# B11+B12 of the fast weight products made by an accumulating DMA in six duos, made first everywhere else, and the last two units of a product swapped

## The chip, the cores and the metric

The kernel runs on one core of one Trainium2 chip. The metric is the device time of one execution in microseconds. Engines are named as the profile names them: PE (TensorE matmul), PEld (its weight load), DVE (VectorE), ACT (ScalarE), POOL (GpSimd), SP (SyncE, which issues nearly all DMAs).

## The reference

A decoder trunk of two layers on 256 tokens, width 2048, in float32. Layer 0 mixes with gated linear attention, layer 1 with differential attention over one shared K/V; each is followed by a SwiGLU feed-forward network (FFN) of width 5632.

```python
def swiglu(h, w_gate_up, w_down):
    gate, up = jnp.split(h @ w_gate_up, 2, axis=-1)
    return (jax.nn.silu(gate) * up) @ w_down
...
        x = x + rmsnorm(mix, post_mix_g[i])
        f = swiglu(rmsnorm(x, pre_ffn_g[i]), ffn_w_gate_up[i], ffn_w_down[i])
        x = x + rmsnorm(f, post_ffn_g[i])
```

## The kernel before, in words

All weights are streamed once from HBM, in pieces of 128 x 1024 floats (512 KB, tile `raw`, line 258). One list, `weight_stream`, gives the order of the whole program. A piece goes through three stations. SP loads it into one of `NRAW` = 5 buffers. ACT rounds it to `hi` (line 294), and DVE subtracts to get `lo` (line 296); both halves go into one of `NRING` = 9 places. PE then makes three products of each pair: a_hi w_hi, a_hi w_lo, a_lo w_hi (lines 370 to 372 and 442 to 444), so that the result has about float32's precision. `pump` converts up to nine pieces ahead of PE and loads up to five pieces ahead of the conversion. The 256 tokens are two blocks of 128.

**Duos.** Where two column chunks c1 and c2 of a weight are computed together (in the FFN: gate chunk c and up chunk 11 + c), some of the eight row pairs s of the chunk are "fast". There the 2 x 2 block product (two token blocks, two column chunks, two row blocks k1, k2) is made in seven block products instead of eight, Strassen-Winograd's way. The fast rows are `FAST_FFN` = 0, 2, 3, 4, 6 (for chunk 1 four of them), and other lists in the mixers. With B11, B21 the halves of the first piece r1 (k1 and k2 of c1) and B12, B22 those of the second piece r2, a fast row gives four units:

- "a": r1 as loaded, two products (banks 0 and 1)
- "b": r2 after the sums, two products (banks 6 and 2)
- "c": r1 after the sums, two products (banks 4 and 3)
- "d": the narrow sum of 128 x 512, one product (bank 5)

The four additions of 128 x 512 run on DVE in `sums` (line 317): B11+B12 over the first half of r1, B12+B22 over the first half of r2, then B11+B12+B22 into the narrow tile `sum`, then that plus B21 over the second half of r1. Behind the last fast row `early` combines banks 0, 5, 6 and 4, and `late` the rest.

**The order on an engine.** The program is recorded in the order of the stream and then put in order by a scheduler that simulates the engines and respects buffers and priorities, so rows of an engine can move when something elsewhere changes. Each engine runs its rows in that order and waits at each for what it needs.

**The stages.** In the trace: gated linear attention (0 to 296 us), its output projection (to 384), FFN 0 (to 1085), values, keys and queries (to 1390), the second output projection `diff_w_out` (to 1468) and FFN 1 with `w_gu1` and `w_d1` (to the end). In an FFN the chunks alternate with down projections. Between the projection and the FFN stands a norm: sums of squares on ACT and DVE, the power -1/2 on POOL (line 625), then transposes on PE and the split of the normed input into `h_ffn` (line 647).

Of the kernel before, what the change touches and what calls it, by code (L numbers as in the profile page):

```python
# [11 lines left out]
F32 = mybir.dt.float32  # L12
# [3 lines left out]
ALU = mybir.AluOpType  # L16
AX = mybir.AxisListType

P = 128
# [3 lines left out]
C = 512  # L23
# [22 lines left out]
CHAIN = (3, 4, 5, 6)  # L46
FIRST_X = {1: [(1, 0), (0, 1)], 3: [(1, 1)], 5: [(0, 2)], 7: [(1, 2)], 9: [(0, 3)], 11: [(1, 3)]}
NRAW, NRING = 5, 9
V_BEGIN, V_EVERY, V_Q = 16, 3, 1


# [29 lines left out]
def weight_stream():  # L81
# [40 lines left out]

    middle_duo("gla_w_out", FAST_OUT)
    ffn(0)
    chunk("w_v", 0)
    chunk("w_v", 3)
    duo(("w_v", 1), ("w_v", 2), FAST_V)
    for name in ("w_k", "diff_w_q"):
        for n in range(KT):
            block(name, n)  # L130
    middle_duo("diff_w_out", FAST_OUT)
    ffn(1)
    return out


def load_list(stream):
    out = []
    for name, idx, kind in stream:
        if kind in ("plain", "beside"):
            out.append((name, idx))  # L140
        elif kind == "a":
            out.extend((name, (n, idx[2])) for name, n in idx[:2])
    return out


class Split:


    def __init__(self, tiles):
        self.tiles = tiles  # L150
# [36 lines left out]
class Trunk:  # L187
    def __init__(self, ctx, tc, t):
        self.ctx, self.tc, self.nc, self.t = ctx, tc, tc.nc, t

        def pool(name, **kw):
            return ctx.enter_context(tc.tile_pool(name=name, bufs=1, **kw))

        self.const = pool("const")
        self.big = pool("big")
        self.ring = pool("ring")
        self.hs = pool("hs")
        self.psum = pool("psum", space=bass.MemoryType.PSUM)
        self.dram = pool("dram", space=bass.MemoryType.DRAM)
        self.n = 0  # L200
        self.later = []
        self.stream = weight_stream()
        self.loads = load_list(self.stream)
        self.n_used = self.n_done = 0
        self.subs = {}
        self.raws = {}
        self.n_dma = self.n_conv = self.n_take = self.n_free = 0
        self.pool_lo = set()
        self.n_narrow = 0
        self.cap = 2  # L210
        self.ident = self.const.tile([P, P], F32, tag="ident", name="ident")
# [44 lines left out]
    def load(self):  # L256
        name, idx = self.loads[self.n_dma]
        raw = self.ring.tile([P, 1024], F32, tag="raw", name=self.uid("raw"), bufs=NRAW)
        self.nc.sync.dma_start(raw, self.t[name][idx])
        self.raws[self.n_dma] = raw  # L260
        self.n_dma += 1

    def raw(self):
# [43 lines left out]
        )  # L307
        return hi

    def sums(self):  # L310

        nc = self.nc
        r1, r2 = self.pending
        t2 = self.narrow[0].tile([P, C], F32, tag="sum", name=self.uid("sum"))

        def add(out, in0, in1):
            nc.vector.tensor_tensor(out=out, in0=in0, in1=in1, op=ALU.add)  # L317

        add(r1[:, :C], r1[:, :C], r2[:, :C])
        add(r2[:, :C], r2[:, :C], r2[:, C:])  # L320
        add(t2, r1[:, :C], r2[:, C:])
        add(r1[:, C:], t2, r1[:, C:])
        self.pending = r1, r2, t2

    def convert(self):
        n = self.n_conv
        kind = self.stream[n][2]
        self.n_done += kind in ("plain", "beside", "c", "b")
        if kind == "plain":
            self.subs[n] = self.split(self.raw(), n in self.pool_lo) if n else self.split_halves(self.raw())  # L330
        elif kind == "beside":
            self.subs[n] = self.split_beside(self.raw())
        elif kind == "a":
            self.pending = self.raw(), self.raw()
            self.subs[n] = self.split(self.pending[0])
        else:
            if kind == "b":
                self.sums()
            self.subs[n] = self.split(self.pending["cbd".index(kind)])
        self.n_conv += 1  # L340

    def pump(self):
# [103 lines left out]
    def duo_act(self, aT, forms, fast, c1, c2, early, late):  # L446

        ps = [self.acc() for _ in range(6)] + [self.tp().rearrange("p j t -> p (j t)")]
        for s in range(8):
            k1, k2 = 2 * s, 2 * s + 1  # L450
            if s in fast:
                f = forms.pairs.index(s)
                plan = {
                    "a": ((0, (k1, 0)), (1, (k2, 0))),
                    "b": ((6, (f, 2)), (2, (f, 3))),
                    "c": ((4, (f, 0)), (3, (k2, 1))),
                    "d": ((5, (f, 1)),),
                }
                first, last = s == fast[0], s == fast[-1]
                for kind, prods in plan.items():  # L460
                    wp = self.take("duo", (c1, c2, s), kind)
                    for j, (bank, (i, which)) in enumerate(prods):
                        plain = kind == "a" or bank == 3
                        a = aT.tokens(i, which) if plain else forms.fast(i, which)
                        stop = last and bank in (0, 5, 6)
                        self.triple(ps[bank], a, wp, j, first, stop)
                    self.free()
                    if kind != "d":
                        self.tick()
                if last:  # L470
                    early(ps)
                continue
            for (w, n), pair in ((c1, ((1, 0), (3, 1))), (c2, ((4, 1), (2, 2)))):
                wp = self.take(w, (n, s))
                for bank, which in pair:
                    for j in range(2):
                        a = forms.diff(k1 + j) if which == 2 else aT.tokens(k1 + j, which)
                        self.triple(ps[bank], a, wp, j, False, s == 7 and j == 1)
                    if s == 7:
                        late(bank, ps)  # L480
                    if bank in (2, 3):
                        self.free()
                    self.tick()

    def duo_apart(self, aT, forms, fast, chunks, early, late):

        ps = {}

        def add(bank, a, wp, j, last):
            first = bank not in ps  # L490
            if first:
                ps[bank] = self.acc() if bank < 6 else self.tp().rearrange("p j t -> p (j t)")
            self.triple(ps[bank], a, wp, j, first, last)

        for s in range(8):
            k1, k2 = 2 * s, 2 * s + 1
            if s not in fast:
                for (w, n), banks in zip(chunks, ((1, 3), (2, 7))):
                    wp = self.take(w, (n, s))
                    for b, bank in enumerate(banks):  # L500
                        for j in range(2):
                            add(bank, aT.tokens(k1 + j, b), wp, j, s == 7 and j == 1)
                        if b:
                            self.free()
                        if s == 7:
                            late(bank, ps)
                        self.tick()
                continue
            f, last = forms.pairs.index(s), s == fast[-1]
            plan = {  # L510
                "a": ((0, aT.tokens(k1, 0)), (1, aT.tokens(k2, 0))),
                "b": ((6, forms.fast(f, 2)), (2, forms.fast(f, 3))),
                "c": ((4, forms.fast(f, 0)), (3, aT.tokens(k2, 1))),
                "d": ((5, forms.fast(f, 1)),),
            }
            for kind, prods in plan.items():
                wp = self.take("duo", (*chunks, s), kind)
                for j, (bank, a) in enumerate(prods):
                    add(bank, a, wp, j, last and bank in (0, 4, 5, 6))
                self.free()  # L520
                if kind != "d":
                    self.tick()
            if last:
                early(ps)
# [632 lines left out]
    def ffn(self, fp, hT, rs, gi, wgu, wd, post, after, name, reload, side=None):  # L1157
        nc = self.nc
        self.narrow, self.n_narrow = (fp, 0, 3), 0
        forms = Forms(FAST_FFN, range(8), self.whole(4, [P, 4, 2, 4, P], f"{name}_fast", F32R))  # L1160
        self.rest_of(forms, 2 * gi + 1, f"{name}_rest")
        temp = self.whole(5, [P, 4, C], f"{name}_temp")
# [48 lines left out]
        f = []  # L1211
# [372 lines left out]
```

## Time and profile before

| | |
|---|---|
| two timed runs | 2179.7 and 2179.91 us, median 2179.8 |
| span of the profiled execution, first to last instruction | 2177.2 us |
| what lies around the span (median less span) | 2.6 us |
| PE, DVE, ACT, POOL busy | 99%, 89%, 58%, 2% |
| DMA engines busy with SP's queue | 60.2% |

The profile gives no time of its own for the profiled execution beside its span, so the runs' median stands for it. Busy PE in this profile is modelled (matmuls overlap), so the number of matmuls in a stretch tells more than the share.

### The profile page before, as it was taken

What the parts mean: (1) busy time and instruction counts of PE and PEld (TensorE: products, weight loads), DVE (VectorE), ACT (ScalarE), POOL (GpSimd) and SP (SyncE); (2) the same over time, 40 slices, a digit from 0 to 9 for tenths busy, and PEclk for the clock granted to TensorE, in tenths of its full rate; (3) what the DMA queues carried; (4) which work ended last, traced back from release to release, by engine and by line L of the source; (5) the groups of instructions that cost most, each with busy time, mean ns of one, the idle gap of its engine ahead of it and who ended that gap; (6) DMA issues with size and microseconds to landing.
All of it is one profiled execution on the core that took longest, in us unless ns stands there. A gap on an engine that the chain in (4) does not pass through costs nothing.

```text
span 2177.2 us, 28399 instructions
## 1 busy us (share of the span) xinstructions
PE 2162.6 (99%) x10098; PEld 1798.1 (83%) x10098; DVE 1932.7 (89%) x2646; ACT 1267.2 (58%) x1744; POOL 35.6 (2%) x66
## 2 busy tenths in 40 slices
PE   9999999999999999999999999999999999999998
PEld 8887788888888888888878888888888888888886
DVE  7989988998999999998898567889999999999986
ACT  8656665665655555554676455556566555555553
POOL 1000000000000000000000000000000000000000
PEclk9999999999999999999999999999999999999999
DMA  8545566666655566665757655465656555666664
GB/s 309 169 149 191 177 228 213 213 221 215 228 176 199 194 213 213 194 224 189 243 187 248 186 174 161 151 235 189 231 194 223 182 185 195 209 206 212 212 213 135
DMA packets 123315, 440.09 MB, mean 202 GB/s; under 512 B 13899, under 2 KB 16628, under 8 KB 121380
## 3 DMA queue, kind: packets, MB, share of 16 engines
q1 hardware_dynamic: 121996, 436.44, 60.2%
q10 hardware_dynamic: 1176, 1.84, 0.3%
q8 instruction: 79, 1.29, 0.2%
q14 instruction: 64, 0.52, 0.1%
HBM read 429.82 MB, written 9.97 MB: 202 GB/s over the span
## 4 chain that ended last, share of the span: by engine, by line
PE 96%; DVE 2%; DMA 1%; issue 1%; ACT 1%; POOL 0%; SPq 0%; DVEq 0%; POOLq 0%; ACTq 0%
PE acc L444 13%; PE acc L443 13%; PE acc L442 13%; PE acc L372 10%; PE acc L370 10%; PE acc L371 10%; PE acc L585 8%; PE acc L586 4%; PE tp L443 3%; PE tp L444 3%; PE tp L442 3%; PE tp L606 1%; DVE lo L296 1%; PE acc L1307 0%; PE acc L1346 0%
## 5 line engine op out<-in xcount | busy, mean ns | idle before, releaser
L294 ACT CAST hi<-raw 128x1024 fp32r<-128x1024 f32 x905 | 929.5, 1051 | 656.6 <-DVE raw L317 272.7
L296 DVE TENSOR_TENSOR lo<-raw,hi 128x1024 fp32r<-128x1024 f32 x903 | 1077.6, 1220 | 151.8 <-ACT hi L294 148.9
L370 PE MATMUL acc<-hi,f_ffn_gT 128*128 128x512 f32 x704 | 274.1, 390 | 0.0
L371 PE MATMUL acc<-lo,f_ffn_gT 128*128 128x512 f32 x704 | 274.0, 390 | 0.0
L372 PE MATMUL acc<-hi,f_ffn_gT 128*128 128x512 f32 x704 | 268.9, 389 | 0.0
L444 PE MATMUL acc<-hi,h_ffn 128*128 128x512 f32 x666 | 259.6, 390 | 0.0
L443 PE MATMUL acc<-lo,h_ffn 128*128 128x512 f32 x666 | 259.2, 389 | 0.0
L442 PE MATMUL acc<-hi,h_ffn 128*128 128x512 f32 x666 | 258.4, 390 | 0.0
L372 PEld LDWEIGHTS acc<-hi,f_ffn_gT 128*128 128x128 f32 x704 | 132.2, 188 | 27.3
L370 PEld LDWEIGHTS acc<-hi,f_ffn_gT 128*128 128x128 f32 x704 | 132.2, 188 | 27.2
L371 PEld LDWEIGHTS acc<-lo,f_ffn_gT 128*128 128x128 f32 x704 | 132.2, 188 | 27.0
L444 PEld LDWEIGHTS acc<-hi,h_ffn 128*128 128x128 f32 x666 | 125.0, 188 | 26.5 <-issue 0.6
L443 PEld LDWEIGHTS acc<-lo,h_ffn 128*128 128x128 f32 x666 | 125.1, 188 | 25.9
L442 PEld LDWEIGHTS acc<-hi,h_ffn 128*128 128x128 f32 x666 | 125.0, 188 | 25.9
L585 PE MATMUL acc<-h_q,hi 128*128 128x512 f32 x256 | 92.5, 401 | 0.0
L585 PE MATMUL acc<-h_kv,hi 128*128 128x512 f32 x256 | 90.6, 399 | 0.0
L585 PE MATMUL acc<-h_mix,hi 128*128 128x512 f32 x256 | 90.5, 398 | 0.0
L317 DVE TENSOR_TENSOR raw<-sum,raw 128x512 f32<-128x512 f32 x122 | 84.2, 690 | 3.5
L317 DVE TENSOR_TENSOR raw<-raw 128x512 f32<-128x512 f32 x122 | 84.2, 690 | 3.3
L317 DVE TENSOR_TENSOR raw<-raw,raw 128x512 f32<-128x512 f32 x122 | 83.9, 687 | 2.0
L317 DVE TENSOR_TENSOR sum<-raw,raw 128x512 f32<-128x512 f32 x122 | 83.5, 684 | 0.0
L586 PE MATMUL acc<-h_q,lo 128*128 128x256 f32 x256 | 73.2, 286 | 0.0
(416 smaller groups left out, 3912.4 us busy)
## 6 DMA issues: line engine op xcount, KB each, us to landing
raw<-in_w_gu_dram SPq DMA_DIRECT2D x352, 512.0 KB, 4.4
raw<-in_w_d_dram SPq DMA_DIRECT2D x176, 512.0 KB, 5.2
raw<-in_gla_w_r_dram SPq DMA_DIRECT2D x32, 512.0 KB, 4.4
raw<-in_gla_w_v_dram SPq DMA_DIRECT2D x32, 512.0 KB, 4.0
raw<-in_gla_w_out_dram SPq DMA_DIRECT2D x32, 512.0 KB, 4.5
raw<-in_w_v_dram SPq DMA_DIRECT2D x32, 512.0 KB, 4.7
raw<-in_w_k_dram SPq DMA_DIRECT2D x32, 512.0 KB, 4.0
raw<-in_diff_w_q_dram SPq DMA_DIRECT2D x32, 512.0 KB, 3.5
```

The source lines that it names most:

```text
L294: nc.scalar.copy(hi, src)
L296: eng.tensor_tensor(out=lo, in0=src, in1=hi.bitcast(F32), op=ALU.subtract)
L317: nc.vector.tensor_tensor(out=out, in0=in0, in1=in1, op=ALU.add)
L370: nc.tensor.matmul(ps, ah, rh, start=(kt == 0), stop=False)
L371: nc.tensor.matmul(ps, ah, rl, start=False, stop=False)
L372: nc.tensor.matmul(ps, al, rh, start=False, stop=(kt == 2 * ns - 1))
L442: nc.tensor.matmul(ps, ah, wh, start=first, stop=False)
L443: nc.tensor.matmul(ps, ah, wl, start=False, stop=False)
L444: nc.tensor.matmul(ps, al, wh, start=False, stop=last)
L585: nc.tensor.matmul(ps, lh, aT.both(kt), start=(kt == 0), stop=False)
L586: nc.tensor.matmul(ps[:, SEQ:], ll, aT.hi(kt), start=False, stop=(kt == KT - 1))
L606: nc.tensor.transpose(tp[:, j, :], src[:, j * P : (j + 1) * P], self.ident)
```

## The change

In the duos of FFN 1 with chunks 2 to 7, the sum B11+B12 is not made by DVE any more. Behind the load of r2 the program issues two more DMAs: SP loads B11 into a narrow tile `sumd` (128 x 512, five buffers), and POOL issues an accumulating DMA that adds B12 from HBM into it. That is 30 fast rows (six duos with five each). Everywhere else DVE makes B11+B12 in kind "a", ahead of the split of r1, in a narrow tile of its own (`sum`, now one buffer in the pool of the ring). The other sums stay in place: B12+B22 in r2, then t1 + B22 over the first half of r1, then that plus B21. So unit "c" now holds B11+B12+B22 where it held B11+B12, and the narrow unit "d" holds B11+B12: the banks 4 and 5 of the two units swap. No matmul is added or removed.

```diff
+SUM_BY_DMA, SUM_CHUNKS = ("w_gu1",), (2, 3, 4, 5, 6, 7)
...
+def summed_loads(stream):
+
+    out, n = {}, 0
+    for name, idx, kind in stream:
+        if kind == "a":
+            (w1, c1), (w2, c2), s = idx
+            if w1 in SUM_BY_DMA and c1 in SUM_CHUNKS:
+                out[n + 1] = ((w1, (c1, s)), (w2, (c2, s)))
+            n += 2
+        elif kind in ("plain", "beside"):
+            n += 1
+    return out
...
         self.raws[self.n_dma] = raw
+        if self.n_dma in self.t1_at:
+            (w1, i1), (w2, i2) = self.t1_at[self.n_dma]
+            t1 = self.more.tile([P, C], F32, tag="sumd", name=self.uid("sumd"), bufs=5)
+            self.nc.sync.dma_start(t1, self.t[w1][i1][:, :C])
+            self.nc.gpsimd.dma_start(t1, self.t[w2][i2][:, :C], accum_op=ALU.add)
+            self.t1s[self.n_dma] = t1
         self.n_dma += 1
...
-    def sums(self):
-
-        nc = self.nc
-        r1, r2 = self.pending
-        t2 = self.narrow[0].tile([P, C], F32, tag="sum", name=self.uid("sum"))
-
-        def add(out, in0, in1):
-            nc.vector.tensor_tensor(out=out, in0=in0, in1=in1, op=ALU.add)
-
-        add(r1[:, :C], r1[:, :C], r2[:, :C])
-        add(r2[:, :C], r2[:, :C], r2[:, C:])
-        add(t2, r1[:, :C], r2[:, C:])
-        add(r1[:, C:], t2, r1[:, C:])
-        self.pending = r1, r2, t2
+    def add(self, out, in0, in1):
+        self.nc.vector.tensor_tensor(out=out, in0=in0, in1=in1, op=ALU.add)
+
+    def convert_fast(self, kind):
+
+        if kind == "a":
+            r1, r2 = self.raw(), self.raw()
+            t1 = self.t1s.pop(self.n_used - 1, None)
+            if t1 is None:
+                t1 = self.ring.tile([P, C], F32, tag="sum", name=self.uid("sum"), bufs=1)
+                self.add(t1, r1[:, :C], r2[:, :C])
+            self.pending = r1, r2, t1
+            return self.split(r1)
+        r1, r2, t1 = self.pending
+        if kind == "b":
+            self.add(r2[:, :C], r2[:, :C], r2[:, C:])
+            self.add(r1[:, :C], t1, r2[:, C:])
+            self.add(r1[:, C:], r1[:, :C], r1[:, C:])
+            return self.split(r2)
+        return self.split(r1 if kind == "c" else t1)
...
-        elif kind == "a":
-            self.pending = self.raw(), self.raw()
-            self.subs[n] = self.split(self.pending[0])
         else:
-            if kind == "b":
-                self.sums()
-            self.subs[n] = self.split(self.pending["cbd".index(kind)])
+            self.subs[n] = self.convert_fast(kind)
...
-                    "c": ((4, (f, 0)), (3, (k2, 1))),
-                    "d": ((5, (f, 1)),),
+                    "c": ((5, (f, 1)), (3, (k2, 1))),
+                    "d": ((4, (f, 0)),),
...
-                "c": ((4, forms.fast(f, 0)), (3, aT.tokens(k2, 1))),
-                "d": ((5, forms.fast(f, 1)),),
+                "c": ((5, forms.fast(f, 1)), (3, aT.tokens(k2, 1))),
+                "d": ((4, forms.fast(f, 0)),),
...
+        self.more = fp
```

The line numbers of the changed kernel are larger: line 296 is 318 there, 317 is 333, and line 625 is 648. Three places show how rows move.

**DVE, one fast row in a summed duo of FFN 1** (the last fast row of chunk 3). Before, with r1 = `raw_14740`, r2 = `raw_14788`:

```order
L317 TENSOR_TENSOR raw_14740<-raw_14740,raw_14788 128x512
L317 TENSOR_TENSOR raw_14788<-raw_14788 128x512
L317 TENSOR_TENSOR sum_14847<-raw_14740,raw_14788 128x512
L317 TENSOR_TENSOR raw_14740<-sum_14847,raw_14740 128x512
L296 TENSOR_TENSOR lo_14853<-raw_14788,hi_14852 128x1024
L296 TENSOR_TENSOR f_ffn_rest<-sum_14847,f_ffn_rest 128x512
L296 TENSOR_TENSOR lo_14862<-raw_14740,hi_14861 128x1024
```

Of the change, with r1 = `raw_14751`, r2 = `raw_14797`:

```order
L333 TENSOR_TENSOR raw_14797<-raw_14797 128x512
L318 TENSOR_TENSOR lo_14850<-raw_14751,hi_14849 128x1024
L318 TENSOR_TENSOR f_ffn_rest<-sumd_14799,f_ffn_rest 128x512
L318 TENSOR_TENSOR lo_14863<-raw_14797,hi_14862 128x1024
L333 TENSOR_TENSOR raw_14751<-sumd_14799,raw_14797 128x512
L333 TENSOR_TENSOR raw_14751<-raw_14751 128x512
L318 TENSOR_TENSOR f_ffn_rest<-sumd_14978,f_ffn_rest 128x512
L318 TENSOR_TENSOR lo_14872<-raw_14751,hi_14871 128x1024
```

Three additions stand where four stood, spread among the splits, and the split of the narrow unit (`f_ffn_rest`, which is taken from `sumd`) has moved ahead of the additions; the one of the next duo's first row (`sumd_14978`) is already here.

**SP and POOL at the end of `diff_w_out`.** SP before, the last loads of that weight and the first of FFN 1's:

```order
L259 DMA raw_12851<-in_diff_w_out_dram 128x1024
L259 DMA raw_12863<-in_diff_w_out_dram 128x1024
L259 DMA raw_12875<-in_diff_w_out_dram 128x1024
L259 DMA raw_12887<-in_w_gu_dram 128x1024
L259 DMA raw_12896<-in_w_gu_dram 128x1024
```

SP of the change, the same place:

```order
L275 DMA raw_12851<-in_diff_w_out_dram 128x1024
L280 DMA sumd_13930<-in_w_gu_dram 128x512
L275 DMA raw_12863<-in_diff_w_out_dram 128x1024
L280 DMA sumd_14028<-in_w_gu_dram 128x512
L280 DMA sumd_14097<-in_w_gu_dram 128x512
L280 DMA sumd_14157<-in_w_gu_dram 128x512
L275 DMA raw_12875<-in_diff_w_out_dram 128x1024
L280 DMA sumd_14275<-in_w_gu_dram 128x512
L275 DMA raw_12887<-in_w_gu_dram 128x1024
L275 DMA raw_12896<-in_w_gu_dram 128x1024
```

POOL before had nothing between the last head's norms (`st_12543`, `st_12548`) and the post-norm of `diff_w_out`; of the change:

```order
L648 TENSOR_TENSOR st_12545<-st_12545,mhalf 128x1
L648 TENSOR_TENSOR st_12550<-st_12550,mhalf 128x1
L281 DMA sumd_13930<-in_w_gu_dram 128x512
L281 DMA sumd_14028<-in_w_gu_dram 128x512
L281 DMA sumd_14097<-in_w_gu_dram 128x512
L281 DMA sumd_14157<-in_w_gu_dram 128x512
L281 DMA sumd_14275<-in_w_gu_dram 128x512
L648 TENSOR_TENSOR st_13060<-st_13060,mhalf 128x1
L648 TENSOR_TENSOR st_13212<-st_13212,mhalf 128x1
L648 TENSOR_TENSOR rs_ffn_0_13318<-st_13319,mhalf 128x1
L648 TENSOR_TENSOR rs_ffn_1_13423<-st_13424,mhalf 128x1
L281 DMA sumd_14454<-in_w_gu_dram 128x512
```

The five tiles of the first summed duo are loaded and summed far ahead of their use, as soon as their memory is free; POOL's two powers of the post-norm (`st_13060`, `st_13212`) now stand behind five accumulating DMAs. Each of the other 25 loads stands where a buffer of the duo before comes free.

**DVE at the start of `diff_w_out`'s duo**, beside the softmax of the last head (`s_0`, `s_1`, the tiles that PE transposes next). Before:

```order
L296 TENSOR_TENSOR lo_12484<-raw_12217,hi_12483 128x1024
L1329 SCALAR_TENSOR_TENSOR s_0_12397<-s_0_12397,st_12399 128x128
L1324 RECIPROCAL st_12408<-st_12408 128x2
L296 TENSOR_TENSOR lo_12510<-raw_12268,hi_12509 128x1024
L1325 TENSOR_TENSOR st_12408<-st_12408,lam_st 128x1
L1326 TENSOR_SCALAR s_1_12406<-s_1_12406,st_12408 128x256
L1329 SCALAR_TENSOR_TENSOR s_1_12406<-s_1_12406,st_12408 128x256
L296 TENSOR_TENSOR lo_12539<-raw_12319,hi_12538 128x1024
```

Of the change, from the same row on, with nine rows of the last two heads left out of the middle (first piece, then second):

```order
L318 TENSOR_TENSOR lo_12484<-raw_12217,hi_12483 128x1024
L333 TENSOR_TENSOR sum_12538<-raw_12319,raw_12381 128x512
L333 TENSOR_TENSOR raw_12381<-raw_12381 128x512
L318 TENSOR_TENSOR lo_12510<-raw_12268,hi_12509 128x1024
L1335 TENSOR_TENSOR s_0_12397<-acc_12394,bias_12347 128x256
L1339 TENSOR_REDUCE st_12399<-s_0_12397 128x2
L1335 TENSOR_TENSOR s_1_12406<-acc_12403,bias_12347 128x512
L644 TENSOR_SCALAR st_12431<-st_12385 128x1
L318 TENSOR_TENSOR f_mix_rest<-sum_12538,f_mix_rest 128x512
```

```order
L1349 TENSOR_TENSOR st_12408<-st_12408,lam_st 128x1
L1350 TENSOR_SCALAR s_1_12406<-s_1_12406,st_12408 128x256
L318 TENSOR_TENSOR lo_12541<-raw_12319,hi_12540 128x1024
L1353 SCALAR_TENSOR_TENSOR s_1_12406<-s_1_12406,st_12408 128x256
```

Two additions, the split of the narrow unit and one wide split have moved ahead of the last step of that softmax, because the sum is now made as soon as both pieces are there.

More of the change, by code (lines that the diff above doesn't have):

```diff
@@ L205, in __init__ @@
         self.subs = {}
+        self.t1s, self.t1_at = {}, summed_loads(self.stream)
         self.raws = {}
```

## The prediction

> **What bounds the kernel now.** I read the page first (span, engines, granted clock, the chain that ended last), then the stretch of FFN 1 in which the change acts, then who waits for whom.
>
> ```profile
> span 2177.2 us, 28399 instructions
> PE 2162.6 (99%) x10098; PEld 1798.1 (83%) x10098; DVE 1932.7 (89%) x2646; ACT 1267.2 (58%) x1744; POOL 35.6 (2%) x66
> PEclk9999999999999999999999999999999999999999
> PE 96%; DVE 2%; DMA 1%; issue 1%; ACT 1%; POOL 0%; SPq 0%; DVEq 0%; POOLq 0%; ACTq 0%
> ```
>
> PE is busy 99% and makes 96% of the chain, at the full granted clock. DVE, with 89%, comes second. Busy PE is modelled, so I ask for the stretch from 1490 to 2150 us (all duos and down projections of FFN 1 but the ends) and for PE's waits over the whole run:
>
> ```profile
> core 0: us, PE busy (x) PEld busy (x) DVE busy (x) ACT busy (x) POOL busy (x), PEclk, DMA share, GB/s
> 1490.00:2150.00 660.00, 660.00 (x2960) 547.41 (x2959) 613.69 (x739) 371.80 (x429) 0.00 (x0) 1.00 0.61 203
> ```
>
> ```profile
> PE acc L372 <- DVE h_ffn L647: 1.2, 4, 0.3
> PE acc L693 <- POOL ones L718: 1.1, 1, 1.1
> PE acc L370 <- ACT h_kv L645: 1.0, 1, 1.0
> PE acc L372 <- DVE h_kv L647: 0.9, 3, 0.4
> PE tp L641 <- DMA x_in<-in_x_dram: 0.7, 1, 0.7
> PE acc L370 <- ACT diff_oT L1370: 0.7, 1, 0.7
> PE acc L371 <- DVE lo L287: 0.2, 1, 0.2
> ```
>
> In 660 us PE issues 2960 matmuls, one per 0.223 us, and the list of waits for that stretch is empty. All of PE's waits in the run are 5.8 us, at the start and at the norms between stages; none is for a sum of a duo. DVE is at 613.69 / 660 = 93%, close, but it isn't waited for.
>
> How far are the conversions ahead of PE?
>
> ```profile
> ACT hi L294 <- DVE raw L317: 126.2, 35, 5.5
> ACT hi L294 <- PE acc L444: 24.9, 16, 3.4
> ACT hi L294 <- PE acc L372: 17.9, 18, 1.7
> ```
>
> 34 times in this stretch ACT waited for PE to free a place, which happens when all nine are full. Nine units hold at least 9 x 6 = 54 matmuls, so a full ring is some 54 x 0.223 = 12 us of work for PE (an estimate; narrow units make it less). ACT's largest wait, 126.2 us for the sums, eats of this lead in the fast rows and never to its end.
>
> **The change part by part.** *1. Thirty additions leave DVE.*
>
> ```profile
> L317 DVE TENSOR_TENSOR sum<-raw,raw 128x512 f32<-128x512 f32 x49 | 33.5, 684 | 0.0
> L296 DVE TENSOR_TENSOR lo<-raw,hi 128x1024 fp32r<-128x1024 f32 x304 | 361.7, 1220 | 32.0 <-ACT hi L294 30.8 <-PE acc L372 0.6
> ```
>
> 30 x 0.684 = 20.5 us of DVE time in six duos. PE waits there 0 us, so on the path this is worth 0. It lengthens the lead of the conversions only. What ends each duo late is next the same as now: PE's own 9966 program matmuls, unchanged.
>
> *2. Thirty plain and thirty accumulating loads, 256 KB each.* SP's part first:
>
> ```profile
> L259 SPq DMA_DIRECT2D raw<-in_w_gu_dram x162: 327/328/776, 1491.1 to 2102.3; - x162
> SPq L259 <- DVE lo L296: 525.6, 244, 9.9
> q1 hardware_dynamic: 121996, 436.44, 60.2%
> gain<-in_post_ffn_g_dram SPq DMA_DIRECT2D x2, 256.0 KB, 3.0
> ```
>
> 30 x 0.33 = 10 us of issuing, on a queue that spends 525.6 us waiting for raw buffers: hidden. The 25 later loads wait for the last reader of a `sumd` buffer, the addition into r1; the split of r1 that frees the next raw buffer stands behind it on DVE, so the raw loads queued behind wait no longer than now. 436.44 MB took 60.2% of 2177 us, so 16 engines move 333 GB/s, and 256 KB take 0.8 us. The accumulation is not in the trace: bounds are 0.8 us of all engines (a plain load, the lowest) and 3.0 us (the 256 KB gain's whole time to landing, the nearest row above); I take 1.6, reading HBM and the tile. Then five fast rows bring 5 x (0.8 + 1.6) = 12 us of DMA work, and a summed duo is 5 x 21 + 3 x 24 = 177 matmuls with 96 of down projections beside it, 273 x 0.223 = 61 us of PE, of which 39%, 24 us, are free. Hidden, and each tile is asked for when the duo before has used it, some 50 us ahead.
>
> *3. The first five, at the end of `diff_w_out`.* Here there is no such room:
>
> ```profile
> 1430.00:1440.00 10.00, 10.00 (x46) 8.29 (x45) 8.62 (x10) 6.32 (x6) 0.00 (x0) 1.00 0.97 356
> 1440.00:1450.00 10.00, 10.00 (x46) 8.29 (x45) 10.00 (x14) 7.08 (x11) 0.00 (x0) 1.00 0.91 320
> 1450.00:1460.00 10.00, 10.00 (x46) 8.29 (x45) 3.80 (x9) 1.37 (x5) 0.00 (x0) 1.00 0.46 163
> 1430.51 8.16 SPq L259 DMA_DIRECT2D raw<-in_diff_w_out_dram  x6
> 1440.08 7.26 SPq L259 DMA_DIRECT2D raw<-in_w_gu_dram  x5
> ```
>
> SP issues them between 1435 and 1440 us into engines that are 97% busy, so their 12 us push the last two `diff_w_out` pieces (by the plain ones ahead of them, 0.8 to 3.3 us, and what the first accumulations take) and the first `w_gu1` pieces (by up to 12 us). The lead of a full ring is 12 us, and the next 10 us use 46% only. I cost it at 0, with 12 us as its bound.
>
> POOL's powers of the post-norm stand behind the five accumulations:
>
> ```profile
> 1403.17 2.46 POOL L625 TENSOR_TENSOR st<-st,mhalf 128x1 f32<-128x1 f32 x2 [13.30 <-DVE st L621]
> 1460.56 0.55 POOL L625 TENSOR_TENSOR st<-st,mhalf 128x1 f32<-128x1 f32 x1 [54.92 <-DVE st L621]
> L296 POOL TENSOR_TENSOR lo<-raw,hi 128x1024 fp32r<-128x1024 f32 x2 | 4.8, 2404 | 12.2 <-ACT hi L294 12.2
> ```
>
> The last plain load, issued by 1440, should land by 1446, so POOL has from about 1440 to 1460.56, 20 us, for five: 4 us each. No row shows what one holds POOL; the bounds are 0.33 (SP's issue) and 2.4 us (POOL's longest instruction), and I take 1, nearer to the first since both issue a DMA. 5 x 2.4 = 12 us still fits. Hidden; uncovered, each us of delay of this power is one of PE, for the transposes of the normed input wait for it.
>
> A rule speaks against issuing here at all. The Trainium skill, "SBUF — State Buffer", section "SBUF: two separate sides", says that GpSimd writes the descriptors of its DMAs over ports that it shares with VectorE, and is shut out while VectorE runs an operation in its two-port mode, f32 copies above all. Two-tensor operations lock it out only against a GpSimd read. By that rule DVE's rows here would not block: they all read two tensors. The trace agrees on the speed: 128 x 1024 take 1220 ns and 128 x 512 take 684, one element each 1.05 ns, no double rate. The time would be the same by both.
>
> *4. The sum first, c and d swapped, everywhere else.* Same additions, same matmuls, rows moved. `early` gets bank 5 three matmuls sooner and bank 4 later, off PE's path. Where PE is close to waiting is the start of `diff_w_out`'s duo:
>
> ```profile
> 1393.88 0.48 DVE L1329 SCALAR_TENSOR_TENSOR s<-s,st 128x256 f32<-128x256 f32 x1
> 1396.90 0.38 PE L1337 MATMUL tp<-ident,s 128*128 128x128 f32 x2
> 1406.62 0.60 PE L1367 MATMUL tp<-ident,hs 128*128 128x128 f32 x4
> 1407.90 0.50 PE L370 MATMUL acc<-hi,diff_oT 128*128 128x512 f32 x1 [0.68 <-ACT diff_oT L1370]
> ```
>
> The last step of the softmax has 1396.90 - 1394.36 = 2.5 us to spare. Two additions and the narrow split (0.68 each, as above) and one wide split (1.22) move ahead of it: 3.3 us, less some overlap, so PE waits up to 0.8 us more, and I take 0.6. At 1407.90 PE now has two matmuls (0.45 us) between the transposes and the matmul that waits 0.68: 0.45 less. Sum 0.6 - 0.45 = +0.2 us, within -0.7 and +2.
>
> Together: 0 + 0 + 0 + 0.2. Against the profiled execution that is a span of 2177.4, and with the 2.6 us around it 2180.0 us.
>
> **The rivals.** *A. The first five collide.* Either POOL is held until each accumulation has landed or the DMA engines take long. The price: with 3.0 to 8.6 us each (the landing of raw pieces below) 15 to 43 us against 20 us of cover, so 0 to 23 us late, 2180 to 2203. It decides from 4 us each. Against it: issuing a DMA holds SP 0.33 us only.
>
> ```profile
> DMA to landing us min/median/max: 3.3/4.5/8.6
> ```
>
> *B. The accumulation saturates the DMA engines*, slower by over 2%. Free are 24 us a duo, so it decides from (24 - 4) / 5 = 4 us of all engines for one. Above, each us costs 5 us a duo, 30 in all; at 5.5 us it is 45 us, 2225, and at 8.6 some 138. For it: the rate of an accumulation is in no row. Against: 4 us would be five times a plain load. The Trainium skill, "DMA: Bandwidth & Descriptors", section "Issuing engines are not separate DMA queues", says POOL's DMAs run on the same 16 engines and interleave, so they get no room of their own; no run so far shows it.
>
> *C. POOL works only in DVE's gaps.* DVE idles 660 - 614 = 46 us here, some 28 in six duos, and 20.5 more without the sums: 1.6 us a sum. At 2.4 us needed it lacks 30 x 0.8 = 24 us, partly covered by the lead: up to +12, 2192. Nothing in the rows shows such a lock. The Trainium skill's rule above speaks against it.
>
> *D. Faster.* Should the moved rows end PE's waits between stages, at most the 5.8 us of the list go; half of it gives 2177. That the sums would not move off DVE is excluded by the order.
>
> **How the numbers follow.** Forecast (within 2.5 us of 2180.0) 0.80; A 0.10, B 0.03, C 0.02, D 0.05. The range 2177.5 to 2187 holds the forecast, part of D, and A up to 7 us late, which bounds the 12 us of DMA work less what the lull after 1450 takes. Two per cent are 43.6 us, about what a measurement of this kernel can tell from no change: slower by more is B and the far end of A, 0.04; faster by more would need eight times PE's waits, 0.01; the rest, 0.95, is within.
>
> **What would show it.** DVE busy falls by 20 us to 1912, with 92 rows of the sum; PE's busy time and count stay; its list of waits from 1490 to 2150 stays empty; POOL's power near 1460 starts within 1 us of now; DMA moves 15.7 MB more. Wrong I am if PE waits for `h_ffn` or `x_mid` near 1465 (A), if ACT waits for raw pieces and PE for `lo` in the summed duos (B), or if DVE's additions wait for `sumd` (C).

## The result, and the profile after

The changed kernel takes 2209.0 us in the median (2206.6 and 2211.5) against 2179.8: a ratio of 1.0135, 95% interval 1.0119 to 1.0152. It is 29 us slower: less than 2%, but an interval clear of 1, and 22 us above the upper end of the predicted range. The profiled execution took 2211.5 us for a span of 2209.8.

From the page of the changed kernel: the span, the engines, the chain that ended last (by engine), three groups of instructions, and the two DMA queues of interest.

```profile
span 2209.8 us, 28456 instructions
PE 2173.9 (98%) x10098; PEld 1801.3 (82%) x10098; DVE 1903.2 (86%) x2616; ACT 1263.9 (57%) x1744; POOL 63.8 (3%) x96
q1 hardware_dynamic: 126316, 444.30, 60.2%
q0 software_dynamic: 4320, 7.87, 2.2%
PE 64%; DVE 18%; DMA 10%; issue 5%; ACT 3%; POOL 0%; DVEq 0%; SPq 0%; ACTq 0%; POOLq 0%
L316 ACT CAST hi<-raw 128x1024 fp32r<-128x1024 f32 x905 | 921.0, 1050 | 668.8 <-DVE raw L333 402.4
L333 DVE TENSOR_TENSOR raw<-raw 128x512 f32<-128x512 f32 x244 | 167.2, 687 | 26.1 <-DMA raw<-in_w_gu_dram 23.5
L333 DVE TENSOR_TENSOR sum<-raw,raw 128x512 f32<-128x512 f32 x92 | 63.3, 688 | 17.0 <-DMA raw<-in_w_gu_dram 8.5
```

The counts are as foreseen: as many matmuls, 92 rows of the sum, 7.87 MB accumulated. But the chain is no longer PE's own: DVE makes 18% of it (2% before) and DMA 10% (1%). The last two rows show the new thing: ahead of its additions DVE now stands idle, 26.1 and 17.0 us in sum, nearly all of it until a raw piece lands (23.5 and 8.5 us for pieces of `w_gu` alone). The largest of PE's waits in the whole run, and some of ACT's and DVE's from 1500 us on (us in total, times, longest):

```profile
PE acc L465 <- ACT hi L316: 7.3, 4, 3.5
PE tp L465 <- ACT f_mix_fast L570: 3.6, 1, 3.6
PE acc L465 <- ACT f_ffn L1224: 3.6, 1, 3.6
PE acc L466 <- DVE lo L318: 2.6, 5, 1.0
```

```profile
ACT hi L316 <- DVE raw L333: 184.9, 62, 6.8
DVE raw L333 <- DMA raw<-in_w_gu_dram: 23.5, 19, 2.8
DVE sum L333 <- DMA raw<-in_w_gu_dram: 3.5, 6, 1.4
```

PE waits in duos, for `hi`, for `lo`, once for the operand `f_mix_fast`, and once for ACT to empty a bank (`f_ffn`). ACT waits 184.9 us for additions where it waited 126.2.

Where is the time lost? I set the start of each k-th matmul of the profiled execution against the same matmul of before (us later, all worked out from the traces):

| matmul | before at | changed | everywhere_only | dma_only | pinned |
|---|---|---|---|---|---|
| 1500 | 306.6 | 0.4 | 0.4 | 0.2 | 0.4 |
| 1800 | 374.3 | 5.8 | 6.2 | 0.2 | 0.0 |
| 3300 (FFN 0) | 707.5 | 6.9 | 7.0 | 0.2 | 0.1 |
| 5100 | 1109.9 | 12.0 | 10.3 | 0.6 | 1.9 |
| 7200 (FFN 1) | 1521.4 | 12.3 | 10.7 | 0.0 | 3.2 |
| 7800 | 1654.8 | 18.3 | 12.1 | 3.4 | 3.7 |
| 8700 | 1856.0 | 27.5 | 15.8 | 17.7 | 3.7 |
| 10080 | 2164.2 | 32.4 | 17.9 | 18.4 | 3.7 |

(The other columns are experiments below.) 12 us go before the first sum by DMA is used, in stages that the change only reorders, and 20 in FFN 1. Of the 12, 5.4 go in one place, which comes next. The 5.1 us between matmuls 3300 and 5100 go in four places, 0.8 to 2.1 us each; 1.8 of them stay in pinned, and no run here takes them apart.

The first loss is at the output projection of the linear attention. The timeline before, one row, and of the change (some rows left out):

```profile
323.83 0.62 ACT L547 CAST f_mix_fast<-f_mix 128x512 fp32r<-128x512 f32 x1 [1.42 <-DVE f_mix L543]
```

```profile
322.30 0.69 DVE L333 TENSOR_TENSOR raw<-raw 128x512 f32<-128x512 f32 x1
322.90 1.22 DVE L318 TENSOR_TENSOR lo<-raw,hi 128x1024 fp32r<-128x1024 f32 x1
324.85 1.22 DVE L318 TENSOR_TENSOR lo<-raw,hi 128x1024 fp32r<-128x1024 f32 x1
327.58 1.22 DVE L318 TENSOR_TENSOR lo<-raw,hi 128x1024 fp32r<-128x1024 f32 x1
329.32 0.68 DVE L333 TENSOR_TENSOR raw<-sum,raw 128x512 f32<-128x512 f32 x1
330.24 1.14 ACT L570 CAST f_mix_fast<-f_mix 128x512 fp32r<-128x512 f32 x2
```

DVE never idles here; additions and splits of the next rows are simply done ahead of the differences from which `f_mix_fast` is cast, and the cast comes 6.4 us later. PE waits 3.6 us for it.

In FFN 1 it looks different. The chain that ended last, around the largest loss (start us, us, what):

```profile
1842.03 1.14 DVE lo L318
1843.16 0.61 DVE raw L333
1843.83 3.68 DMA raw<-in_w_gu_dram
1848.14 1.23 DVE lo L318
1849.41 0.80 PE acc L466
```

A raw piece's landing stands in the chain, between an addition and a split. How such a wait reaches PE shows best at the other large loss, near 1660 us (DVE's and ACT's timeline, some rows left out):

```profile
1653.32 0.69 DVE L333 TENSOR_TENSOR raw<-raw 128x512 f32<-128x512 f32 x1 [1.41 <-DMA raw<-in_w_gu_dram]
1660.61 1.29 DVE L333 TENSOR_TENSOR raw<-raw 128x512 f32<-128x512 f32 x2 [1.33 <-DMA raw<-in_w_gu_dram]
1662.01 1.04 ACT L316 CAST hi<-raw 128x1024 fp32r<-128x1024 f32 x1 [6.79 <-DVE raw L333]
1662.96 1.07 ACT L1224 COPY f_ffn<-acc 128x512 f32<-128x512 f32 x2
```

Twice DVE stands at an addition until r2 has landed. In the chain that ended last these two landings stand in series (4.45 and 5.41 us): the split behind the first addition frees the buffer of the second load. ACT waits 6.79 us for the addition, its copy that empties a bank stands behind that, and PE waits 3.6 us for the bank.

In DVE's queue of the changed kernel B12+B22, which needs only r2, now stands ahead of the splits of older pieces: of the 30 rows summed by DMA, 28 have it ahead of r1's own split (by 1 to 9 rows). In 24 it stands three to six rows behind the instruction that frees r2's buffer, while a piece of `w_gu` takes 4.3 us to land in the median. (These counts go by the program's order and the addresses of its buffers: 77 of the 122 r2 take the buffer of the load four before. The counts of rows behind a freeing in the expectations below take it to be five before, and are off by some rows.) Before, no addition of the 122 fast rows stood ahead of its r1's split, since the first of them wrote r1's left half and had to wait until the split had read it. That tie went when B11+B12 got a tile of its own.

### The profile page after: what moved, and what is told of

Its sections match the earlier page's. It is cut to its first block, busy times and chain, and to the rows that moved or that the text cites. A ratio compares the mean times of both kernels' runs of the same rounds, so it can differ in the third digit from the quotient of the medians.

```text
span 2209.8 us, 28456 instructions
## 1 busy us (share of the span) xinstructions
PE 2173.9 (98%) x10098; PEld 1801.3 (82%) x10098; DVE 1903.2 (86%) x2616; ACT 1263.9 (57%) x1744; POOL 63.8 (3%) x96
## 3 DMA queue, kind: packets, MB, share of 16 engines
q0 software_dynamic: 4320, 7.87, 2.2%
## 4 chain that ended last, share of the span: by engine, by line
PE 64%; DVE 18%; DMA 10%; issue 5%; ACT 3%; POOL 0%; DVEq 0%; SPq 0%; ACTq 0%; POOLq 0%
DVE lo L318 9%; PE acc L608 8%; PE acc L466 8%; PE acc L467 8%; PE acc L465 8%; PE acc L393 7%; PE acc L395 7%; PE acc L394 7%; DMA raw<-in_w_gu_dram 5%; PE acc L609 4%; DMA raw<-in_w_d_dram 4%; DVE raw L333 3%; ACT hi L316 2%; PE tp L465 2%; PE tp L466 2%
## 5 line engine op out<-in xcount | busy, mean ns | idle before, releaser
L333 DVE TENSOR_TENSOR raw<-raw 128x512 f32<-128x512 f32 x244 | 167.2, 687 | 26.1 <-DMA raw<-in_w_gu_dram 23.5
L316 ACT CAST f_ffn_rest<-sum 128x512 fp32r<-128x512 f32 x68 | 42.1, 619 | 62.7 <-DVE sum L333 59.5
L333 DVE TENSOR_TENSOR sum<-raw,raw 128x512 f32<-128x512 f32 x92 | 63.3, 688 | 17.0 <-DMA raw<-in_w_gu_dram 8.5
L609 PE MATMUL acc<-h_mix,lo 128*128 128x256 f32 x256 | 71.5, 279 | 0.0
```

Of the source, the lines that this page charges most:

```text
L316: nc.scalar.copy(hi, src)
L333: self.nc.vector.tensor_tensor(out=out, in0=in0, in1=in1, op=ALU.add)
L609: nc.tensor.matmul(ps[:, SEQ:], ll, aT.hi(kt), start=False, stop=(kt == KT - 1))
```

## The experiments

Theory at the outset: **queue order**. The moved additions lost their tie to r1's split, and DVE, which works its queue in order, does them or waits for them ahead of work that PE needs sooner. Rivals: the DMA work (engines, SP's queue), and the swap of c and d.

**everywhere_only**: the whole change without sums by DMA.

```diff
-SUM_BY_DMA, SUM_CHUNKS = ("w_gu1",), (2, 3, 4, 5, 6, 7)
+SUM_BY_DMA, SUM_CHUNKS = (), ()
```

> The sum first and c/d swapped everywhere, but no sum by DMA: VectorE keeps all 92 sums B11+B12. Theory (order on VectorE's queue: additions that need only the second raw piece now stand ahead of splits of older pieces and hold the queue until that piece lands): about 12 us before FFN 1 as in the changed kernel, and in FFN 1 at least FFN 0's 8 us since all its additions are there: 2200, within 2194 to 2212. Rival (the 20 us of FFN 1 come from the DMA traffic, its queues or its waits): only the 12 us stay, 2192. Rival of the prediction's step 4 (moved rows cost nothing): 2180.

2199.3 us, ratio 1.0092 (1.0078 to 1.0106): two thirds of the loss come without any sum by DMA, 10.7 us before FFN 1 and 7.2 within.

**dma_only**: new code in the six duos alone. There units c and d hold the sums of the changed kernel but keep the operands and banks of before, so each sum meets the other's operand in the other's bank and the products are not those that the combination needs; number and size of all instructions are those of the change there.

```diff
+            self.pending = (r1, r2) if t1 is None else (r1, r2, t1)
+            self.old = t1 is None
...
+        if self.old:
+            if kind == "b":
+                self.sums()
+            return self.split(self.pending["cbd".index(kind)])
```

> The six duos with sums by DMA as in the changed kernel, every other duo with the order and layout of before. Theory (queue order): nothing is lost before FFN 1 (span offset 0 +- 1 us at its start), and of the 20 us in FFN 1 some 15 to 20 stay, since 15 of the additions of the second piece stand there one row behind the split that frees its buffer: 2195 to 2200. Rival (the loss in FFN 1 was carried in from the stages before): under 2185.

2196.3 us, 1.0078 (1.0065 to 1.0091). Nothing before FFN 1, 18.4 us within: that loss is made there and not carried in.

**idle_dma**: the kernel before plus the 60 loads into unread tiles.

```diff
+        if self.n_dma in self.t1_at:
+            (w1, i1), (w2, i2) = self.t1_at[self.n_dma]
+            t1 = self.more.tile([P, C], F32, tag="sumd", name=self.uid("sumd"), bufs=5)
+            self.nc.sync.dma_start(t1, self.t[w1][i1][:, :C])
+            self.nc.gpsimd.dma_start(t1, self.t[w2][i2][:, :C], accum_op=ALU.add)
```

> The kernel before, with the 30 plain and 30 accumulating loads into tiles that nobody reads; all additions as before. Theory (queue order): the DMA work itself is hidden, as the prediction's step 2 has it: 2180 to 2182. Rival (DMA traffic delays raw pieces, or SyncE's queue is held by the sum tiles): most of the 20 us of FFN 1, 2195 to 2200.

2188.7 us, 1.0046 (1.0033 to 1.0060): between the two. Most of it, 7.8 of 9.3 us, is lost in one place, between 1521 and 1588 us of the kernel before. SP's and PE's waits in this kernel there:

```profile
SPq L280 <- DMA sumd<-in_w_gu_dram: 24.9, 9, 6.0
PE acc L463 <- ACT hi L315: 3.9, 1, 3.9
```

SP, with the raw loads behind it, stood nine times before an accumulation that had still to land: an unread tile is free at once and taken again. That is a cost of this experiment's own design; read_dma checks it.

**pinned**: the whole change and a tie.

```diff
+            self.nc.vector.scalar_tensor_tensor(
+                out=r2[:, :1], in0=self.pending[3][:, :1].bitcast(F32), scalar=0.0, in1=r2[:, :1],
+                op0=ALU.mult, op1=ALU.add,
+            )
```

(`self.pending[3]` is r1's lo; B11+B12 by DVE follows it.)

> The whole change, with one tiny VectorE instruction per fast row (adds 0 times an element of r1's lo to one element of r2) that ties the additions behind r1's split; DMA sums, layout and swap stay. Theory (queue order): the loss goes, 2180 to 2185, and VectorE no longer waits for a raw piece in an addition. Rival (DMA traffic): 2195 to 2200 by FFN 1's share. Rival (the c/d swap, by the order in which banks 4 and 5 end): the 12 us before FFN 1 stay, 2190 or more.

2183.1 us, 1.0017 (1.0009 to 1.0026): 25 of the 29 us are gone, with everything else of the change in place. From its page:

```profile
L333 DVE TENSOR_TENSOR raw<-raw 128x512 f32<-128x512 f32 x244 | 165.1, 685 | 2.6
```

The idle time ahead of these additions fell from 26.1 to 2.6 us. That the position of the additions behind or ahead of r1's split is the cause is shown.

**pinned_no_dma**: the same tie in everywhere_only (same edit).

> As everywhere_only (no sum by DMA, sum into a narrow tile of its own, c and d swapped), with the tie that puts all additions of a fast row behind r1's split. Theory (queue order): 2179 to 2183; of the 10.7 us that everywhere_only has at the start of FFN 1, at most the 2 us that the pinned kernel has there stay. Rival (the swap of c and d): near 10 us stay, 2190.

2183.1 us, 1.0017 (1.0008 to 1.0026), at the upper end of the expected range. Of the 10.7 us at FFN 1's start 2.9 stay, more than the 2 expected. The swap is not the cause of the loss; what of the remaining 3.7 us is swap and what the 122 tie instructions was not separated.

**read_dma**: idle_dma with one reader per tile.

```diff
+            nc.vector.scalar_tensor_tensor(
+                out=t2[:, :1], in0=self.t1[:, :1], scalar=0.0, in1=t2[:, :1], op0=ALU.mult, op1=ALU.add
+            )
```

> The kernel before with the 30 plain and 30 accumulating loads, as idle_dma, but each tile is read by one tiny VectorE instruction (0 times an element of it is added to one of the row's sum), so that a tile stays taken until its row is converted and SyncE's next load of such a tile has another buffer. If idle_dma's 7.8 us came from SyncE's queue standing behind accumulations into a tile taken again at once (24.9 us of such waits there): 2179 to 2181. Rival (the DMA traffic itself): 2187 to 2189 again.

2181.6 us, 1.0011 (1.0001 to 1.0020), just above the expected 2179 to 2181. The traffic, together with its 30 tiny readers, costs about 2 us.

**dma_only_pinned**: sums by DMA in six duos, with their c and d swapped, and the tie (edit as in pinned).

> Sums by DMA in the six duos with c and d swapped there, their additions tied behind r1's split; order and layout of before everywhere else. Theory (queue order): 2179 to 2181, the time of before although VectorE does 30 additions less, as the prediction's step 1 has it. Rival (DMA traffic): 2187 or more. Rival (relief of VectorE pays): under 2176.

2181.7 us, 1.0010 (1.0001 to 1.0019), just above the expected 2179 to 2181. With 30 additions less on DVE the kernel is no faster. No version here beats the kernel before.

The next runs ask what it is about the position: **A**, the additions are done ahead of more urgent splits, or **B**, DVE stands still for r2's landing with older splits behind it.

**touch_second**: before, with a copy of one element of r2 that waits for its landing.

```diff
+        if self.n_dma in self.seconds:
+            self.nc.vector.tensor_copy(raw[:, :1], raw[:, :1])
```

> The kernel before with one more VectorE instruction per fast row: it copies one element of the second raw piece onto itself, with no link to the split of the first. It stands two or three rows behind the split that frees the buffer. If the wait for the landing in VectorE's queue is itself what costs: three rows of 1.22 us against some 4.5 us to landing leave 1 us of hold in some 50 rows, of which part is paid: 2182 to 2195. If it is only that half-microsecond additions are done ahead of more urgent rows: 2179 to 2181.

2183.4 us, 1.0024 (1.0015 to 1.0032). At the low end of the first reading: DVE stood still a good deal (table below), and it cost little.

**forms_urgent**: everywhere_only with the operands of the output projections at high priority.

```diff
-                self.defer(1 + 3 * j, step)
+                self.defer(1 + 3 * j, self.urgent(step))
```

> everywhere_only with one line more: in the two output projections the operands of the fast rows (f_mix and f_mix_fast) are issued at high priority, so that VectorE's queue has them ahead of the splits and additions that everywhere_only put before them; the additions of the weights stay as early as there. Theory (VectorE, full, does moved additions ahead of what PE needs next): the 3.6 us wait for f_mix_fast goes, and of the 5.8 us lost between the 1500th and the 1800th matmul under 1.5 stay; the rest as everywhere_only, 2192 to 2196. Rival (raw pieces come late there): 5 to 6 us stay, 2199.

2200.6 us, 1.0092 (1.0077 to 1.0107), the 6.2 us at matmul 1800 unchanged. But DVE's order at the linear attention's projection came out the same row for row; the priority moved only rows of the second projection. The run doesn't test what it was meant to.

**pinned_half**: the whole change, tied to the lo before the row.

```diff
+            self.nc.vector.scalar_tensor_tensor(
+                out=r2[:, :1], in0=self.last[:, :1].bitcast(F32), scalar=0.0, in1=r2[:, :1],
+                op0=ALU.mult, op1=ALU.add,
+            )
```

> The whole change, with the tie to the lo of the unit split just before the row in place of r1's own. In VectorE's queue the additions of 45 of the 122 rows still stand ahead of their own r1's split (182 rows ahead in sum), against 109 (491) in the changed kernel and none in pinned; they stand three rows or more behind the split that frees the buffer. Theory A (additions done ahead of older splits cost, whether or not a piece is waited for): in proportion to the rows ahead, 3.8 + 26 x 182 / 491 = 13 us over before, 2188 to 2197. Theory B (only the standing still until the piece lands costs): 2182 to 2185 as pinned.

2190.8 us, 1.0053 (1.0036 to 1.0069). The time is A's, but the premise failed: the tie itself waited for landings, 19.7 us in FFN 1. It doesn't part A from B.

**early_work**: dma_only_pinned with 30 additions that nobody needs.

```diff
+            r1 = self.raws[self.n_dma - 1]
+            spare = self.more.tile([P, C], F32, tag="spare", name=self.uid("spare"), bufs=1)
+            self.add(spare, r1[:, :C], r1[:, C:])
```

> dma_only_pinned with 30 extra additions of 128x512 on VectorE (into a tile nobody reads, from the first raw piece, which has landed by then), one per fast row of the six duos: they stand 1 to 15 rows ahead of the row's own r1 split and at least five rows behind the split that freed their buffer, so they bring early work and no standing still. Four sum tiles in place of five, for room. Theory A (work done ahead of older splits costs): most of the 18 us that dma_only has in FFN 1, 2192 to 2200. Theory B (it is the standing still until a piece lands): 2181 to 2184.

2199.7 us, 1.0086 (1.0072 to 1.0101). Again A's time, and again the premise failed: these additions waited 23.0 us for r1's landing, though each stands four rows or more behind the instruction that frees r1's buffer.

**hold_older**: before, all additions in place; the lo of an older unit waits for r2.

```diff
+            nc.vector.scalar_tensor_tensor(
+                out=hi[:, :1], in0=self.held[:, :1], scalar=0.0, in1=hi[:, :1].bitcast(F32),
+                op0=ALU.mult, op1=ALU.add,
+            )
```

> The kernel before, with 30 tiny VectorE instructions in the six duos: each adds 0 times an element of the second raw piece of a row to one element of the hi of the next unit that is split after that piece's load is issued, so that the lo of an older unit stands in VectorE's queue behind the landing of a newer piece; 18 of them come right behind the split that frees its buffer. All additions as before. Theory B (standing still ahead of older splits costs): 2188 to 2200. Theory A (only additions done early cost): 2179 to 2183.

2241.5 us, 1.0286 (1.0271 to 1.0300): B, and far more of it than expected, since the waits were longer than I had reckoned. The tie holds more than the lo, though: it writes the older unit's hi, so PE has to wait for that too (12.9 us in FFN 1, in the list of PE's waits). DVE's waits for raw pieces from 1500 us on, one row each of touch_second, pinned_half, dma_only, early_work and hold_older:

```profile
DVE raw L274 <- DMA raw<-in_w_gu_dram: 16.8, 14, 1.9
```

```profile
DVE raw L341 <- DMA raw<-in_w_gu_dram: 19.7, 13, 3.3
```

```profile
DVE raw L333 <- DMA raw<-in_w_gu_dram: 23.4, 20, 2.1
```

```profile
DVE spare L336 <- DMA raw<-in_w_gu_dram: 23.0, 13, 3.9
```

```profile
DVE hi L314 <- DMA raw<-in_w_gu_dram: 69.4, 29, 3.9
```

Beside what each loses in FFN 1 (from matmul 7200 to 10080):

| kernel | DVE stands still for raw, us | lost in FFN 1, us | per us |
|---|---|---|---|
| pinned, dma_only_pinned | no row | 0.5, 1.6 | |
| touch_second | 16.8 | 3.7 | 0.22 |
| pinned_half | 19.7 | 6.5 | 0.33 |
| dma_only | 23.4 | 18.4 | 0.79 |
| early_work | 23.0 | 19.2 | 0.83 |
| changed | 27.0 (23.5 + 3.5) | 20.1 | 0.74 |
| hold_older | 69.4 | 62.1 | 0.89 |

In four kernels the loss is 0.7 to 0.9 us for each microsecond that DVE stands still, and one of them, hold_older, moves no addition at all. So in FFN 1 standing still ahead of older splits can make a loss of this size without any addition moved; how much of hold_older's comes by its tie on hi was not separated. The ratio is an average and no price of a single wait: in the changed kernel 17.0 of the 20.1 us go in three stretches of 60 matmuls (from the 7740th, the 8520th and the 9060th), where DVE stands still for 4 us, and the other 23 us of standing still cost 3. What they do to the conversions' lead over PE before a stretch in which it runs out is argued, not shown. Where the wait stands nearer its own row (in FFN 1, 26 of 49 touches are one or two rows ahead of r1's split, and half of pinned_half's ties stand behind it), the loss per microsecond is 0.2 to 0.3 us; that this distance is the reason is argued, not shown. Whether additions done early cost anything in FFN 1 by themselves stays open, because none of the runs had them without the waits; everywhere_only loses 7.2 us there with only 4.7 us of waiting, which says they may. Before FFN 1 they do: the 5.4 us at the linear attention's projection go with a wait of 0.5 us for the raw pieces of that weight, and pinning removes them.

## Why the prediction was wrong

**The step that failed is step 4**, "Same additions, same matmuls, rows moved", priced at +0.2 us with +2 as its end. everywhere_only, which is that step with 30 DVE sums more, costs 20 us. I looked for its price at one place, the start of `diff_w_out`'s duo (where the changed kernel loses 1.8 us between matmuls 6300 and 6900), and went by the number of additions, not by what each row may wait for. The row that tells it stood in the order: `raw_14797<-raw_14797` ahead of the split of `raw_14751`, r2's addition ahead of r1's split. The question not asked was what had held it back before. In its place the runs show that the moved rows cost 19.9 us without a sum by DMA, and that a tie that moves them back behind r1's split takes 25 of the change's 29 us away.

**Step 1** was right in its worth and wrong in its ending. Thirty additions less on DVE are worth nothing: dma_only_pinned (2181.7 us) takes the time of read_dma (2181.6 us), which has the same loads and all additions. But "What ends each duo late is next the same as now" assumed that DVE's queue kept its order. DVE busy came to 1903.2 us for the 1912 foreseen, and the list of PE's waits in FFN 1 isn't empty.

**Step 2** held. The accumulating queue takes 2.2% of 16 engines' span, 0.022 x 2209.8 / 30 = 1.6 us for each, the value taken, which was a guess between two bounds that came out; hidden but for some 2 us (read_dma). That the sum tiles don't hold SP was wrong as said and right in its worth: SP stands 21.5 us at them in FFN 1 of the changed kernel, until DVE's additions free one, but 58.9 us in dma_only_pinned, which loses 1.6 us there. Only idle_dma, where the tiles were taken again too soon, lost by it, 7.8 us.

**Step 3** held too. POOL's part, from the timeline of the changed kernel:

```profile
1452.15 1.04 POOL L281 DMA_DIRECT2D sumd<-in_w_gu_dram  x1 [38.85 <-DVE hs L1089]
1463.02 0.89 POOL L281 DMA_DIRECT2D sumd<-in_w_gu_dram  x1 [1.73 <-issue]
1473.06 0.56 POOL L648 TENSOR_TENSOR st<-st,mhalf 128x1 f32<-128x1 f32 x1 [9.15 <-DVE st L644]
```

An accumulation holds POOL 0.9 to 1.1 us (1 was taken, again a choice between bounds), and the power waits for DVE's `st`, not for the DMAs; it is 12.5 us later only because the stage is 12 us later. Between matmuls 6600 and 7200 the change loses 1.5 us and everywhere_only, without these loads, 1.6.

**The rivals**: A, B and C, each for one resource of the DMA sums, are not what happened. B's sign did appear, PE waiting for `lo` in the summed duos, but with the DMA engines busy 68% of FFN 1 and only 2 us to their account. A rival "the moved rows stand ahead of what PE needs" was missing. The order allowed an estimate: with 1.14 us for each wide row and 0.60 for each narrow one between the freeing of r2's buffer and B12+B22 (start to start in DVE's timeline) and 4.3 us to landing, the 30 rows summed by DMA stand still for some 36 us (23.5 were waited).

## What to carry to other kernels

When a change gives a value a buffer of its own, ask which write-after-read it takes away: that accidental tie may be all that keeps an early-ready instruction behind the urgent ones in an in-order queue. Read the order for each moved row as "what does it wait for, and what stands behind it", above all where it waits for a load into a buffer freed only a few rows ahead. If it stands wrong, one tiny instruction that makes a true dependency puts it back (25 of 29 us here, for 0 times an element).

## What was unexpected of the hardware

A stop of PE costs more than its length. Stretches of the changed kernel around the stop at 1659.6 us, with the columns of such a view in the prediction (length; busy time of PE, PEld, DVE, ACT and POOL; granted clock; share of the DMA engines; GB/s):

```profile
1659.00:1664.00 5.00, 1.41 (x7) 0.86 (x6) 2.48 (x4) 1.99 (x4) 0.88 (x1) 1.00 0.82 310
1664.00:1668.00 4.00, 4.00 (x13) 3.18 (x12) 3.90 (x6) 3.41 (x6) 0.00 (x0) 0.63 0.82 197
1668.00:1672.00 4.00, 4.00 (x18) 3.23 (x18) 3.43 (x5) 2.00 (x2) 0.00 (x0) 0.94 0.58 197
```

After 3.98 us from one matmul's start to the next the granted clock falls to 0.63 in the next 4 us, and seven matmuls start 0.427 us apart in place of some 0.23: 7 x 0.2 = 1.4 us more. All five stops of 3.7 us or more in the changed kernel, everywhere_only and idle_dma are followed by such a run; of the stops of 1.9 to 3.2 us in the runs here only some are (one of 2.2 us in dma_only is, by seven). The Trainium skill, "TensorE: Matmul & The Clock Gate", section "Part 1: The HAM clock gate", says that the array's clock halves after about 3.4 us of idleness, seen in windows that run free of the program. The trace agrees on the long stops and, with 0.427 us for some 0.23, on a spacing nearly doubled; that stops of 2.2 us can do it too is the trace's own.
